# A transformer block with sixteen experts on one core: small operations moved to other places in the order, and permuted copies written contiguously

## The chip, the cores and the metric

The kernel runs on one core of a Trainium2 chip. The metric is the device time of one execution of the whole program, in microseconds (us); of several executions the median is given. A core has five engines that run side by side and wait for each other through semaphores: PE (the matrix engine, TensorE), DVE (VectorE), ACT (ScalarE), POOL (GpSimd) and SP (SyncE), which here issues nearly all transfers (DMAs) from the chip's memory. Matrix products land in PSUM, an accumulator memory that the program uses as eight banks of 128 x 512 floats; everything else lies in SBUF. Each engine works through its own instructions in the order in which the program has put them there, so an instruction that waits holds up all behind it on that engine.

## The reference

One block over 256 tokens of 1024 numbers, all in float32: a norm, one wide projection, two kinds of attention side by side, gates, an output projection, and then a mixture of experts. Cut to what matters:

```python
h = rms_norm(x, norm_mix_g)
(f_q, f_k, f_v, f_f, n_q, k_c, v_c, k_s, v_s, k_w, v_w, n_g, g_a, g_b) = split_cols(h @ w_in)   # 1024 x 4896
out_a = fox_attention(rms_norm(f_q), rms_norm(f_k), f_v, log_sigmoid(f_f + b_forget)) @ w_fox_up
kc = rms_norm(compress_blocks(k_c, ...))        # 15 blocks of 32 tokens, two layers with gelu
vc = compress_blocks(v_c, ...)
out_b = nsa_attention(rms_norm(n_q), kc, vc, rms_norm(k_s), v_s, rms_norm(k_w), v_w, sigmoid(n_g)) @ w_nsa_up
x = x + (sigmoid(g_a) * out_a + sigmoid(g_b) * out_b) @ w_out
...
# experts: 4 groups of 4; each token takes its best group, and the best two experts in it
hid = silu(einsum('td,edf->etf', t, w_gate)) * einsum('td,edf->etf', t, w_up)      # 1024 x 512 each
hid = hid * combine.T[:, :, None]
x = x + einsum('etf,efd->td', hid, w_down)                                         # 512 x 1024 each
```

The weights of the sixteen experts are 16 x 3 x 2 MB; each is read once.

## The kernel before

**Precision.** Before the experts, most operands are split into two parts, a rounded one (names with H) and the remainder (names with L), and a product is the sum of three products of parts. ACT makes the rounded part of a weight piece (`hi`, L173), DVE the remainder (`lo`, L179).

**Projection.** The weight matrix goes by in pieces of 2 x 512 columns. `go` issues half a piece's products (six matmuls on PE), `load` fetches a piece some steps ahead, and `hi` and `lo` split an earlier one. `half_a` is `go`, `lo`, `load` and then whatever functions it is given; `half_b` is `go`, `hi` and then its functions. So the functions of a `half_a` are issued behind a weight remainder on DVE. `k_scaled` (L753) is such a function: it scales the keys by their norms, twice, and `kk_turn` (L730) transposes the result on PE.

**Compressed keys and values.** `g_turn`, `c_in`, `c_root`, `c_turn`, `c_scores` and so on are short steps that are put between the attention's units. `c_in` forms keys and values of the compressed blocks in one PSUM bank, and ACT sums the keys' squares from there. `c_root` takes the root on DVE in a chain of small instructions, scales the keys (`kcn`, L836) and spreads the values over heads (`vblk`, L837), both out of that bank, which stays taken until then. `bank(...)` hands out banks by name; there are two of the name tp, in turn. An attention unit's scores are scaled by DVE (L579) and turned by PE (L587) into a bank tp.

**Tokens for the experts.** The tokens' rows are kept in permuted order as `xH` and `xL` (L1060 by ACT, L1063 by DVE; `by_row` and `eights` give the views): element q * 8 + k of a row goes to k * 128 + q, so that a slice of 128 columns is what one k step of a product wants. The products hid are permuted in the same way, by four.

**Experts' loop.** The experts go in eight pairs (here the first to the eighth; `pr` 0 to 7 in the code), each expert with up to 64 places for tokens, so that a pair fills the 128 columns of a product. `proj` (L1347) forms the gate or the up product of a pair: for each of eight k steps one matmul for either expert, and behind the fourth it calls the functions in `between`, half way. For each pair there are, in the order as written before:

- the gate product; half way through the up product `ready` for the next pair: one-hot matrices on DVE (L1007), `slots` (six small matmuls L1326 into a bank tp, and from it L1329 to L1331 on DVE, into `j6` and `csl`), and `rows` (two transposes and a copy of the one-hots on DVE, L1338 to L1340, in a bank tp too);
- `silu` on ACT (L1393, L1397), and the product hid on DVE (L1399), from the up product's bank;
- the scatter of the pair before (L1357, L1358) into four banks `acc` that hold the sum over all pairs;
- the turn: four transposes of hid (L1408) and their copy hdT on ACT (L1409);
- in every second pair the gather of the next two pairs' tokens (L1317, scaled by DVE, L1318);
- the down products (L1373), their results split into the parts of `y` by ACT and DVE (L1361, L1362);
- the issue of twelve more weight loads on SP;
- in the third and fifth pair four sums of `xH` and `xL` into `acc` on DVE (L1430), which add the block's input to the result.

The first pair's gate product is formed ahead of the loop. The second pair's `rows` and `ready` stand in its gate product's middle instead.

**Loads.** Expert weights come in tiles of 1 MB through SP's queue, first in, first out, into a ring of places; a load waits until the tile that lay in its place has been used, and the loads behind it wait with it.

**Order.** Within the loop the block `manual_schedule(engines={PE})` keeps PE's instructions as written; the order on DVE and ACT is chosen by the compiler's scheduler. For the eighth pair, `last_pair`, all engines keep the written order.

## Time and profile before

| | us |
|---|---|
| median of three runs | 451.19 |
| lowest and highest of them | 451.06, 453.54 |
| the profiled execution's own time | 451.66 |
| its span in the trace | 449.7 |
| PE busy in it | 430.3 |
| DVE busy in it | 214.7 |
| ACT busy in it | 167.0 |

The span is the stretch from the first recorded instruction to the last. Busy times are those in which an engine works; they overlap between engines. In rows of a timeline the first number is the start, in us from the span's start, the second the busy time of the row; then engine, line, operation, output<-inputs by the program's names, shapes, and the number of instructions that the row joins. A bracket at the end gives the idle time of the engine just ahead of the row and the instruction that ended it. In rows of groups, the numbers behind the bar are busy time in us, mean ns of one, and the idle time ahead of them with what ended most of it. The expert part of the program runs from some 225 us to the end.

### The profile page before, as it was taken

The page shows a single profiled execution, that of the slowest core. Times are in us where ns is not written, and L with a number is a line of the kernel's source. Part 1 is how long each engine was busy: PE and PEld are TensorE (multiplying, and loading weights), DVE is VectorE, ACT ScalarE, POOL GpSimd, SP SyncE. Part 2 cuts the span into 40 slices and gives each one's busy share as a digit, 9 for nine tenths or more (in the row PEclk, how much of TensorE's full clock was granted, in tenths as well). Part 3 has the DMA queues.
Part 4 walks back from the last instruction along what each step waited for, and adds up shares of the span by engine and source line. Part 5 has one row for each costly group of instructions (what it writes and reads, how often), then busy time and mean ns, then how long its engine had stood idle before and what let it go on. Part 6 is the DMA issues. An engine that isn't in the chain of part 4 may idle for free.

```text
span 449.7 us, 6356 instructions
## 1 busy us (share of the span) xinstructions
PE 430.3 (96%) x2370; PEld 258.9 (58%) x2370; DVE 214.7 (48%) x611; ACT 167.0 (37%) x343; POOL 10.5 (2%) x25
## 2 busy tenths in 40 slices
PE   7998999999999999999999899989999999999994
PEld 4895766767777777878952336333363335433443
DVE  5869776797856565576654224133130512201012
ACT  4786563957767665534732100101011010101011
POOL 8000000000000000000000000000000000000000
PEclk8999999999999999999999999999999999999998
DMA  8699643656763439999889999799999999999922
GB/s 285 131 366 303 216 138 95 222 183 214 254 206 94 129 109 351 408 408 374 352 310 335 351 391 422 280 422 421 420 420 418 420 420 418 422 418 416 391 78 98
DMA packets 41425, 136.10 MB, mean 303 GB/s; under 512 B 7296, under 2 KB 12976, under 8 KB 30384
## 3 DMA queue, kind: packets, MB, share of 16 engines
q1 hardware_dynamic: 41248, 135.54, 80.3%
q8 instruction: 20, 0.33, 0.3%
q10 hardware_dynamic: 144, 0.13, 0.1%
q14 instruction: 13, 0.11, 0.1%
HBM read 134.61 MB, written 1.05 MB: 302 GB/s over the span
## 4 chain that ended last, share of the span: by engine, by line


## 5 line engine op out<-in xcount | busy, mean ns | idle before, releaser
L1347 PE MATMUL z<-m,xg 128*64 128x512 f32 x432 | 100.5, 595 | 0.0
L179 DVE TENSOR_TENSOR wL<-raw,wH 128x1024 fp32r<-128x1024 f32 x48 | 58.4, 1220 | 12.2 <-ACT wH L173 12.0
L173 ACT ACTIVATE wH<-raw 128x1024 fp32r<-128x1024 f32 x48 | 50.5, 1056 | 36.8 <-PE z L201 21.5
L1347 PEld LDWEIGHTS z<-m,xg 128*64 128x64 f32 x432 | 31.5, 137 | 56.5 <-issue 54.6
L199 PE MATMUL z<-wH,hH 128*128 128x512 f32 x128 | 54.4, 425 | 0.0
L200 PE MATMUL z<-wL,hH 128*128 128x512 f32 x128 | 50.4, 393 | 0.0
L201 PE MATMUL z<-wH,hL 128*128 128x512 f32 x128 | 50.3, 393 | 0.0
L1373 PE MATMUL tp<-m,gh 128*64 128x512 f32 (+1 forms) x208 | 49.5, 580 | 0.7 <-ACT gh L1409 0.7
L1373 PEld LDWEIGHTS tp<-m,gh 128*64 128x64 f32 x208 | 15.8, 137 | 28.8 <-issue 25.7
L199 PEld LDWEIGHTS z<-wH,hH 128*128 128x128 f32 x128 | 24.1, 188 | 11.4 <-issue 7.1
L1361 ACT ACTIVATE y<-tp 128x512 fp32r<-128x512 f32 (+1 forms) x15 | 8.6, 583 | 56.7 <-PE tp L1373 56.6
L1340 DVE CAST ST<-tp 128x256 fp32r<-128x256 bf16 x8 | 3.4, 423 | 54.7 <-PE tp L1338 54.7
L1362 DVE TENSOR_TENSOR y<-tp,y 128x512 fp32r<-128x512 f32 (+1 forms) x15 | 10.0, 673 | 36.7 <-ACT y L1361 36.7
L201 PEld LDWEIGHTS z<-wH,hL 128*128 128x128 f32 x128 | 24.1, 188 | 5.5
L1409 ACT ACTIVATE gh<-tp 128x512 f32<-128x512 f32 x7 | 4.2, 598 | 59.6 <-PE tp L1408 59.6
L200 PEld LDWEIGHTS z<-wL,hH 128*128 128x128 f32 x128 | 24.2, 189 | 3.7
L570 ACT ACTIVATE sc<-sc,mx 128x128 f32<-128x128 f32 (+1 forms) x48 | 21.2, 445 | 1.7 <-DVE mx L564 1.4
L1393 ACT ACTIVATE gh<-z,csl 128x512 f32<-128x512 f32 x6 | 4.1, 688 | 39.2 <-PE z L1347 39.2
L1399 DVE SCALAR_TENSOR_TENSOR gh<-gh,csl,z 128x512 f32<-128x512 f32 x7 | 7.9, 1128 | 20.8 <-PE z L1347 15.1
L579 DVE TENSOR_SCALAR sc<-sc,sm 128x128 f32<-128x128 f32 (+1 forms) x48 | 12.1, 316 | 0.4
L1317 PE MATMUL tp<-one,xH 128*128 128x256 f32 x48 | 12.3, 297 | 0.0
L587 PE MATMUL tp<-ident,sc 128*128 128x128 f32 x72 | 10.5, 278 | 1.8 <-DVE vblk L837 1.0
(423 smaller groups left out, 701.5 us busy)
## 6 DMA issues: line engine op xcount, KB each, us to landing
m<-in_w_gate SPq DMA_DIRECT2D x29, 1024.0 KB, 17.2
m<-in_w_up SPq DMA_DIRECT2D x28, 1024.0 KB, 11.5
m<-in_w_down SPq DMA_DIRECT2D x22, 1024.0 KB, 12.5
raw<-in_w_in SPq DMA_DIRECT2D x36, 512.0 KB, 4.6
m<-in_w_down SPq DMA_DIRECT2D x10, 512.0 KB, 9.4
raw<-in_w_out SPq DMA_DIRECT2D x8, 512.0 KB, 10.3
m<-in_cmp_k_w SPq DMA_DIRECT2D x8, 256.0 KB, 8.5
m<-in_cmp_v_w SPq DMA_DIRECT2D x8, 256.0 KB, 4.8
```

Source lines behind the costliest of these rows:

```text
L173: A.activation(P["H"], P["raw"], AF.Copy)
L179: (eng or V).tensor_tensor(P["L"], P["raw"], P["H"].bitcast(F32), op=ALU.subtract)
L199: T.matmul(p[t], lH[k // 4][:, k % 4, ts], P["H"][:, k - k0], start=(k == 0), stop=False)
L200: T.matmul(p[t], lH[k // 4][:, k % 4, ts], P["L"][:, k - k0], start=False, stop=False)
L201: T.matmul(p[t], lL[k // 4][:, k % 4, ts], P["H"][:, k - k0], start=False, stop=(k == K - 1))
L570: A.activation(sc, sc, AF.Exp, scale=-1.0, bias=u["mx"][:, i, t:t + 1], accum_out=u["sm"][:, i, t:t + 1])
L579: V.tensor_scalar(sc, sc, u["sm"][:, i, t:t + 1], None, op0=ALU.mult)
L587: T.transpose(p[:, 128 * j:128 * j + 128], u["sc"][i][:, 128 * j:128 * j + 128], ident)
L1317: T.matmul(p[:, j], X[t][:, cs], Sr[:, t], start=(i == 0), stop=(i == 3))
L1347: T.matmul(p[64 * i:64 * i + 64], xg[:, k, o + 64 * i:o + 64 * i + 64], w[k // 4][:, k % 4], start=(k == 0), stop=(k == 7), tile_position= ...
L1362: V.tensor_tensor(yHL[:, 1, c0:c0 + n], p[:, 0:n], yHL[:, 0, c0:c0 + n].bitcast(F32), op=ALU.subtract)
L1373: T.matmul(p[64 * i:64 * i + 64, 0:n], hdT[:, f, 64 * i:64 * i + 64], w, start=(f == 0), stop=(f == 3), tile_position=(0, 64 * i))
```

## The change

It has six parts. Lines are those of the changed program where it says so.

1. `k_scaled` is issued ahead of the weight remainder instead of behind it.
2. In `c_in`, ACT copies the compressed keys out of the bank into a new tile `kcr`, and DVE forms `vblk` there; `c_root` then scales `kcr`, and no longer reads the bank.
3. The views of the permuted copies go the other way: the elements are visited in the order of the permuted tile, so it is written (or, in the sums into `acc`, read) contiguously, and the other operands, sums in PSUM among them, with a step of 8 or 4 floats. This concerns `xH`, `xL`, hid and the sums into `acc`. The same elements are computed.
4. `csl` and `j6` get two buffers each.
5. In the first pair the gate product of the second pair stands between hid and the down products, with the turn in its middle. The second pair then has only an up product in front of hid; `rows` of the first pair stands at its middle, and `ready` with `silu` of the second pair behind its sixth k step. The one-hots of the third pair are formed there too, but its `slots` and `rows` only behind the gather.
6. The loop's `manual_schedule` holds DVE and ACT in the written order as well.

```diff
@@ -766 @@
-        half_a(k_scaled)
+        go()
+        k_scaled()
+        lo()
+        load()
@@ c_in @@
-            p = pw[0] = bank([128, 512], "tp")
+            p = bank([128, 512], "tp")
...
             A.activation(ks_, p[0:32, 0:64], AF.Square, accum_out=kcst[:, 0:1])
+            A.activation(kcr, p[0:32, 0:64], AF.Copy)
+            V.tensor_tensor(vblk, p[:, None, 64:128].to_broadcast([128, 8, 64]), hm[:, :, None].to_broadcast([128, 8, 64]), op=ALU.mult)
@@ c_root @@
-            V.tensor_scalar(kcn, pw[0][0:32, None, 0:64].to_broadcast([32, 2, 64]), kcst[:, 1:2], None, op0=ALU.mult)
-            V.tensor_tensor(vblk, pw[0][:, None, 64:128].to_broadcast([128, 8, 64]), hm[:, :, None].to_broadcast([128, 8, 64]), op=ALU.mult)
+            V.tensor_scalar(kcn, kcr[:, None, :].to_broadcast([32, 2, 64]), kcst[:, 1:2], None, op0=ALU.mult)
@@ by_row, eights @@
-        return X.rearrange("p (k q) -> p q k", k=8)[:, c0 // 8:c1 // 8]
+        return X.rearrange("p (k q) -> p k q", k=8)[:, :, c0 // 8:c1 // 8]
...
-        return X[:, c0:c1].rearrange("p (q k) -> p q k", k=8)
+        return X[:, c0:c1].rearrange("p (q k) -> p k q", k=8)
@@ slots @@
-        c = wk.tile([128, 3], F32, name="csl")
-        j6 = wk.tile([128, 6], F32, name="j6")
+        c = wk.tile([128, 3], F32, name="csl", bufs=2)
+        j6 = wk.tile([128, 6], F32, name="j6", bufs=2)
@@ proj @@
-    def proj(w0, w1, xg, o, between=()):
+    def proj(w0, w1, xg, o, between=(), after=()):
...
+            if k == 5:
+                for f in after:
+                    f()
@@ expert_pair @@
-        if pr:
-            pg = proj(tiles[2 * pr, 0], tiles[2 * pr + 1, 0], xg, o, pre0)
-            pre0.clear()
+        if pr == 1:
+
+            pu = proj(tiles[2, 1], tiles[3, 1], xg, o, pre0, [lambda: (pre.append(ready(1)()), silu(pg0[1], pre[0][0])),
+                                                               lambda: later.append(ready(2))])
+            c, Sb, ST = pre.pop(0)
+        elif pr:
+            pg = proj(tiles[2 * pr, 0], tiles[2 * pr + 1, 0], xg, o)
             c, Sb, ST = pre.pop()
-            A.activation(sg, pg, AF.Silu, scale=c[:, 1:2])
-        pu = proj(tiles[2 * pr, 1], tiles[2 * pr + 1, 1], xg, o, [lambda: pre.append(ready(pr + (pr > 0))())])
-        if pr == 0:
+            silu(pg, c)
+            pu = proj(tiles[2 * pr, 1], tiles[2 * pr + 1, 1], xg, o, [lambda: pre.append(ready(pr + 1)())])
+        else:
+            pu = proj(tiles[0, 1], tiles[1, 1], xg, o, [lambda: pre.append(ready(0)())])
             c, Sb, ST = pre.pop()
-            A.activation(sg, pg0, AF.Silu, scale=c[:, 1:2])
-        fours = lambda h: h.rearrange("p (q k) -> p q k", k=4)
-        V.scalar_tensor_tensor(hid.rearrange("p (k q) -> p q k", k=4), fours(sg), c[:, 2:3], fours(pu), op0=ALU.mult, op1=ALU.mult)
+            silu(pg0[0], c)
+        fours = lambda h: h.rearrange("p (q k) -> p k q", k=4)
+        V.scalar_tensor_tensor(hid.rearrange("p (k q) -> p k q", k=4), fours(sg), c[:, 2:3], fours(pu), op0=ALU.mult, op1=ALU.mult)
...
+        if pr == 0:
+            pg0.append(proj(tiles[2, 0], tiles[3, 0], xg, 128, [turn]))
+        else:
+            turn()
...
         if pr % 2 == 1:
             xgs[pr // 2 + 1] = gather(pr // 2 + 1)
+        if later:
+            pre.append(later.pop()())
...
-                        o = acc[t][hf].rearrange("p (q k) -> p q k", k=8)
+                        o = acc[t][hf].rearrange("p (q k) -> p k q", k=8)
...
-            pre0.extend([lambda: got.append(rows(Sb)), lambda: pre.append(ready(1)())])
+            pre0.append(lambda: got.append(rows(Sb)))
@@ the loop @@
-    with tc.manual_schedule(engines={mybir.EngineType.PE}):
+    with tc.manual_schedule(engines={mybir.EngineType.PE, mybir.EngineType.DVE, mybir.EngineType.Activation}):
```

How the instructions stand on an engine in the two programs, at three places; a name with a number is one tile of that name, and x2 or x4 joins equal rows.

On DVE at the compressed keys, before, from the copy of the hidden layer to the next weight remainder; `kcst` and `rs_u` are the root's small tiles, `sm` and `sc` those of an attention unit's softmax:

```order
L808 TENSOR_SCALAR hT<-tp_843 128x128
L809 COPY hTv<-hT 128x256
L573 RECIPROCAL sm<-sm 128x4
L575 TENSOR_TENSOR sm<-sm,ngate 128x4
L579 TENSOR_SCALAR sc<-sc,sm 128x128
...
L834 TENSOR_SCALAR kcst<-kcst 32x1
...
L836 TENSOR_SCALAR kcn<-tp_859,kcst 32x128
L837 TENSOR_TENSOR vblk<-tp_859,hm 128x512
L179 TENSOR_TENSOR wL<-raw,wH 128x1024
```

And in the changed program:

```order
L810 TENSOR_SCALAR hT<-tp_844 128x128
L811 COPY hTv<-hT 128x256
L179 TENSOR_TENSOR wL<-raw,wH 128x1024
L821 TENSOR_TENSOR vblk<-tp_860,hm 128x512
L573 RECIPROCAL sm<-sm 128x4
L575 TENSOR_TENSOR sm<-sm,ngate 128x4
L579 TENSOR_SCALAR sc<-sc,sm 128x128
...
L839 TENSOR_SCALAR kcst<-kcst 32x1
```

`vblk` now stands ahead of the attention unit's scaling, and the last reader of its bank is no longer behind the root's chain.

On PE in the first pair, before: z is the bank of a gate or up product, m and wl are weight tiles, gh is the tile that holds sg, hid and hdT, and tp a bank for turns and down products.

```order
L1347 MATMUL z_2670<-m_2033,xg 64x512
L1347 MATMUL z_2670<-m_2055,xg 64x512
L1408 MATMUL tp_2704<-ident,gh 128x128 x4
L1373 MATMUL tp_2711<-m_2077,gh 64x512
L1373 MATMUL tp_2711<-m_2099,gh 64x512
...
L1347 MATMUL z_2761<-m_2121,xg 64x512
L1347 MATMUL z_2761<-m_2145,xg 64x512
```

And in the changed program:

```order
L1351 MATMUL z_2672<-m_2035,xg 64x512
L1351 MATMUL z_2672<-m_2057,xg 64x512
L1351 MATMUL z_2706<-m_2123,xg 64x512
L1351 MATMUL z_2706<-m_2147,xg 64x512
...
L1427 MATMUL tp_2715<-ident,gh 128x128 x4
L1351 MATMUL z_2706<-m_2176,xg 64x512
L1351 MATMUL z_2706<-m_2207,xg 64x512
...
L1380 MATMUL tp_2730<-m_2079,gh 64x512
L1380 MATMUL tp_2730<-m_2101,gh 64x512
```

Half of the second pair's gate product (eight matmuls) now stands on each side of the turn; the down products follow behind its second half.

On DVE in the third pair, before: `ST` is the copy of `rows`, one_3095 the one-hots of the fourth pair, gh<-gh,csl,z the product hid, and o and s banks of `acc`.

```order
L1340 CAST ST<-tp_2989 128x256
L1007 TENSOR_TENSOR one_3095<-slot,rank__2607 128x128 x2
L1399 SCALAR_TENSOR_TENSOR gh<-gh,csl,z_2965 128x128x4
L1430 TENSOR_TENSOR o_2663<-o_2663,xH_2221 128x512
L1329 ISA j_2985,csl<-tp_2977,half 128x6
L1329 ISA csl 128x1
L1330 TENSOR_REDUCE csl<-tp_2977 128x1
L1430 TENSOR_TENSOR o_2663<-o_2663,xL_2222 128x512
L1331 TENSOR_TENSOR csl<-csl 128x1
```

And in the changed program:

```order
L1333 ISA j_2987,csl<-tp_2979,half 128x6
L1333 ISA csl 128x1
L1334 TENSOR_REDUCE csl<-tp_2979 128x1
L1335 TENSOR_TENSOR csl<-csl 128x1
L1344 CAST ST<-tp_2991 128x256
L1416 SCALAR_TENSOR_TENSOR gh<-gh,csl,z_2967 128x512
L1369 TENSOR_TENSOR y<-tp_3020,y 128x512
L1369 TENSOR_TENSOR y<-tp_3031,y 128x512
L1456 TENSOR_TENSOR o_2665<-o_2665,xH_2223 128x8x64
L1456 TENSOR_TENSOR o_2665<-o_2665,xL_2224 128x8x64
```

The reads of `slots`'s bank (`j6` and `csl`) moved from behind hid to ahead of it, and the sums into `acc` from between them to behind the parts of `y`; the fourth pair's one-hots now stand behind those sums.

More of the change, by code (lines that the diff above doesn't have):

```diff
@@ L801, in block_kernel @@
         hTv = at.tile([128, 2, 2, 4, 16], F32, name="hTv")
-        pw = {}
         def g_turn():
@@ L831, in block_kernel @@
         ks_ = wk.tile([32, 64], F32, name="kcs", bufs=1)
+        kcr = wk.tile([32, 64], F32, name="kcr", bufs=1)
         def c_root():
@@ L1385, in ready, with silu @@
         return rest_
+    def silu(pg, c):
+        A.activation(sg, pg, AF.Silu, scale=c[:, 1:2])
+    pg0, later = [pg0], []
     def expert_pair(pr, pend):
         xg, o = xgs[pr // 2], pr % 2 * 128
-        if pr:
-            pg = proj(tiles[2 * pr, 0], tiles[2 * pr + 1, 0], xg, o, pre0)
-            pre0.clear()
+        if pr == 1:
[4 more added lines that the diff above has]
+            pg = proj(tiles[2 * pr, 0], tiles[2 * pr + 1, 0], xg, o)
             c, Sb, ST = pre.pop()
-            A.activation(sg, pg, AF.Silu, scale=c[:, 1:2])
-        pu = proj(tiles[2 * pr, 1], tiles[2 * pr + 1, 1], xg, o, [lambda: pre.append(ready(pr + (pr > 0))())])
-        if pr == 0:
+            silu(pg, c)
+            pu = proj(tiles[2 * pr, 1], tiles[2 * pr + 1, 1], xg, o, [lambda: pre.append(ready(pr + 1)())])
+        else:
+            pu = proj(tiles[0, 1], tiles[1, 1], xg, o, [lambda: pre.append(ready(0)())])
             c, Sb, ST = pre.pop()
-            A.activation(sg, pg0, AF.Silu, scale=c[:, 1:2])
-        fours = lambda h: h.rearrange("p (q k) -> p q k", k=4)
-        V.scalar_tensor_tensor(hid.rearrange("p (k q) -> p q k", k=4), fours(sg), c[:, 2:3], fours(pu), op0=ALU.mult, op1=ALU.mult)
+            silu(pg0[0], c)
+        fours = lambda h: h.rearrange("p (q k) -> p k q", k=4)
+        V.scalar_tensor_tensor(hid.rearrange("p (k q) -> p k q", k=4), fours(sg), c[:, 2:3], fours(pu), op0=ALU.mult, op1=ALU.mult)
         if pr == 1:
@@ L1405, in expert_pair, with turn @@
             scatter(*pend, 512, 512, pr == 1)
-        p = bank([128, 4, 128], "tp")
-        for f in range(4):
-            T.transpose(p[:, f], hid[:, f * 128:f * 128 + 128], ident)
-        A.activation(hdT, p, AF.Copy)
+        def turn():
+            p = bank([128, 4, 128], "tp")
+            for f in range(4):
+                T.transpose(p[:, f], hid[:, f * 128:f * 128 + 128], ident)
+            A.activation(hdT, p, AF.Copy)
+        if pr == 0:
+            pg0.append(proj(tiles[2, 0], tiles[3, 0], xg, 128, [turn]))
+        else:
+            turn()
         if pend and pr % 2 == 0:
```

## The prediction

> **What bounds it now.** First the page's busy shares, then its clock and bandwidth rows, to see which engine could set the end at all.
>
> ```profile
> span 449.7 us, 6356 instructions
> PE 430.3 (96%) x2370; PEld 258.9 (58%) x2370; DVE 214.7 (48%) x611; ACT 167.0 (37%) x343; POOL 10.5 (2%) x25
> PEclk8999999999999999999999999999999999999998
> GB/s 285 131 366 303 216 138 95 222 183 214 254 206 94 129 109 351 408 408 374 352 310 335 351 391 422 280 422 421 420 420 418 420 420 418 422 418 416 391 78 98
> ```
>
> PE is busy 96% at the full clock, so time is won only where PE stands still, or by doing less on it; this change takes nothing off PE. The bandwidth stands flat near 420 GB/s from slice 26 (292 us) on, so the weights might set the end instead. The DMA view by stretches gives 15.1 us from issue to landing for the last pieces of the eighth pair's up weights; the timeline gives the issue and the use:
>
> ```profile
> m<-in_w_up SPq DMA_DIRECT2D x3, 512.0 KB, 15.1
> 405.19 0.33 SPq L107 DMA_DIRECT2D m<-in_w_up  x1
> 429.47 1.03 PE L1450 MATMUL z<-m,xg 128*64 128x256 f32 x8
> ```
>
> The piece lands at 405.2 + 15.1 = 420.3 and is used at 429.5: 9.2 us of slack. PE, not the DMA, sets the end, and up to about 9 us can be taken from PE before weights are late. So I went through PE's timeline for rows with idle time in brackets. Behind 40 us there are few; these are the ones near the edited lines:
>
> ```profile
> 42.84 0.66 PE L730 MATMUL tp<-ident,m 128*128 128x128 f32 x4 [1.16 <-DVE m L753]
> 67.67 0.52 PE L587 MATMUL tp<-ident,sc 128*128 128x128 f32 x3 [1.05 <-DVE vblk L837]
> 228.82 0.36 PE L1213 MATMUL s<-one,xH 128*128 128x256 f32 x1 [1.08 <-DVE one L1007]
> 247.89 0.66 PE L1408 MATMUL tp<-ident,gh 128*128 128x128 f32 x4 [1.28 <-DVE gh L1399]
> 249.23 1.94 PE L1373 MATMUL tp<-m,gh 128*64 128x512 f32 x8 [0.69 <-ACT gh L1409]
> 260.69 0.48 PE L1326 MATMUL tp<-cb,one 128*128 128x3 bf16 x6 [0.72 <-DVE one L1007]
> 302.38 0.63 PE L1408 MATMUL tp<-ident,gh 128*128 128x128 f32 x4 [1.27 <-DVE csl L1330]
> 354.60 0.63 PE L1408 MATMUL tp<-ident,gh 128*128 128x128 f32 x4 [0.55 <-DVE csl L1330]
> 406.80 0.63 PE L1408 MATMUL tp<-ident,gh 128*128 128x128 f32 x4 [0.53 <-DVE csl L1330]
> ```
>
> They sum to 8.33 us, and the change touches all nine. A wait costs about 0.1 us more than its bracket, since an unhindered matmul starts before the modelled end of the last.
>
> **The change, part by part.**
>
> *(a) The scaled keys ahead of the weight remainder.* At 42.84 PE waits for the two L753 products, which stand behind an L179:
>
> ```profile
> 40.37 1.22 DVE L179 TENSOR_TENSOR wL<-raw,wH 128x1024 fp32r<-128x1024 f32 x1
> 41.50 1.29 DVE L753 TENSOR_TENSOR m<-kraw,krs 128x512 f32<-128x512 f32 x2
> ```
>
> Swapped, the products end at about 41.7, where PE comes free (42.84 - 1.16 = 41.68). Left is some 0.15 for the handover: 1.16 + 0.1 - 0.15 = **1.1 us** gained. The L179 ends 1.3 us later; its piece is consumed two pieces on, so nobody waits. The load behind it waits for an older remainder.
>
> *(b) The compressed keys and values.* At 67.67 the second turn waits for a PSUM bank that `c_root` still reads:
>
> ```profile
> 62.81 0.66 PE L816 MATMUL tp<-w,hTv 128*128 128x64 f32 x4
> 63.61 1.01 DVE L579 TENSOR_SCALAR sc<-sc,sm 128x128 f32<-128x128 f32 x4
> 63.74 0.18 ACT L817 ACTIVATION_READ_ACCUMULATOR kcs<-tp 32x1 f32 x1
> 66.13 0.49 PE L587 MATMUL tp<-ident,sc 128*128 128x128 f32 x3
> 66.85 0.67 DVE L837 TENSOR_TENSOR vblk<-tp,hm 128x512 f32<-128x512 f32 x1
> 72.32 1.07 PE L851 MATMUL tp<-nqT,kcT 64*32 64x256 f32 x16
> ```
>
> Now ACT copies the keys (a 32-row copy, some 0.2 us as its square beside it) and DVE forms vblk straight behind it, 64.15 to 64.85. The bank is free 2.7 us sooner. But vblk now stands ahead of the score scaling, and what is behind it on DVE waits: scaling ends near 66.3 instead of 64.62. PE's second turn would start near 66.45, so it just fits. The root chain, the next remainder and the next scores move 0.6 us later; PE, 1.15 us earlier, meets them at the compressed scores (72.32), where I leave 0.15. Gain 1.05 + 0.1 - 0.15 = **1.0 us**.
>
> *(c) xH and xL, hid, and the sums into acc: contiguous writes, strided reads.* Their present prices, and the contiguous neighbour:
>
> ```profile
> L1399 DVE SCALAR_TENSOR_TENSOR gh<-gh,csl,z 128x512 f32<-128x512 f32 x7 | 7.9, 1128 | 20.8 <-PE z L1347 15.1 <-issue 5.7
> L1063 DVE TENSOR_TENSOR xL<-x,xH 128x512 fp32r<-128x512 f32 x4 | 4.2, 1078 | 0.6 <-ACT xH L1060 0.6
> L1430 DVE TENSOR_TENSOR s<-s,xH 128x512 f32<-128x512 f32 x2 | 2.1, 1050 | 0.3 <-PE s L1358 0.3
> L1362 DVE TENSOR_TENSOR y<-tp,y 128x512 fp32r<-128x512 f32 x14 | 9.6, 690 | 36.7 <-ACT y L1361 36.7
> ```
>
> L1399 has one strided side, the write. L1430 has one too, but it is a read (xH; acc and output are contiguous), and costs as much. L1063 has both and still costs 1.08. So a stride costs about 0.4 us whichever side has it, and not twice. No row shows a read with a step of 4 or 8 floats, nor any strided PSUM operand. The price therefore lies between 0.69 (the step is free) and 0.69 + 2 x 0.44 = 1.57 us (hid's two strided inputs add up). I take **unchanged**, 1.13 and 1.05: L1430 is the nearest row, being a strided read. Then the wait at 228.82, behind two L1063 (2 x 1.08) and a one-hot, stays: **0**. At 0.69 it gives 2 x 0.39 = 0.78.
>
> The Trainium skill, Vector Engine (DVE) Microarchitecture Reference, section 5.2, speaks against the edit: it measured streams that hop every element at about 1.7 ns a column and small steps of 24 words at 2.5, with "more for small non-adjacent steps than for large ones". By its figures hid would take an estimated 512 x 2.5 + 75 ns = 1.36 us and the whole sum below would be near 4.8 us. The strided L1399 here comes to 1128 / 512 = 2.2 ns a column all in, with a step of 128 words; nothing here shows a small step.
>
> *(d) First pair.* The second pair's gate product is put behind hid, with the turn in its middle.
>
> ```profile
> 246.75 1.08 DVE L1399 SCALAR_TENSOR_TENSOR gh<-gh,csl,z 128x512 f32<-128x512 f32 x1 [3.25 <-PE z L1347]
> 248.59 0.60 ACT L1409 ACTIVATE gh<-tp 128x512 f32<-128x512 f32 x1 [4.50 <-PE tp L1408]
> 256.15 3.60 PE L1347 MATMUL z<-m,xg 128*64 128x512 f32 x16
> ```
>
> The last row is half a product (four of eight k): 3.44 us without its tail. hid (1.1) now runs beside the first half and the hdT copy (0.60 plus handover) beside the second; even at 1.57 hid is covered. Both waits go: 1.28 + 0.69 + 0.2 = **2.2 us**. The same matmuls are done. If that cover were gone, the two waits would be back whole. The SP queue keeps its order; the first pair's down slots come free about 2.5 us later in it and hold the loads queued behind, out of a slack of 9.
>
> *(e) Second pair.* The wait for a one-hot at 260.69 goes, because four k steps' half (1.7 us) now lies between the cast and it: +0.72 + 0.1. In its place `slots` and `rows` of the third pair now follow the gather and use the same two banks. `rows` waits for the gather's last scaling and the down product for the j6 reads:
>
> ```profile
> L1318 DVE TENSOR_TENSOR xg<-tp,g_row 128x512 f32<-128x512 f32 x12 | 8.3, 691 | 7.9 <-PE tp L1317 7.9
> 302.07 0.16 DVE L1330 TENSOR_REDUCE csl<-tp 128x1 f32<-128x3 f32 x1
> ```
>
> Scaling ends 0.15 + 0.69 behind the gather, `slots` covers 0.3: 0.6 with handover, then 0.2 for the reads. Lost 0.8; net **0**.
>
> *(f) Third, fifth and seventh pair.* j6 and csl stood behind hid (single buffer), at the third behind an acc sum as well, and the turn needs their bank:
>
> ```profile
> 300.12 1.13 DVE L1399 SCALAR_TENSOR_TENSOR gh<-gh,csl,z 128x512 f32<-128x512 f32 x1 [2.85 <-issue]
> 300.71 0.40 PE L1358 MATMUL s<-y,ST 128*128 128x512 f32 x1
> ```
>
> With two buffers and DVE in written order they run before hid; only hid is left. It ends at 301.25, PE could go at 300.71 + 0.23: 0.35 left with handover, at each of three. 1.27 + 0.55 + 0.53 + 0.3 - 3 x 0.35 = **1.6 us**; at hid 0.69 all 2.65, at 1.57 some 0.3.
>
> *(g) Written order on DVE.* At the fourth and sixth pair the one-hots now queue behind four acc sums:
>
> ```profile
> 310.78 7.04 PE L1347 MATMUL z<-m,xg 128*64 128x512 f32 x32
> 311.65 0.69 DVE L1362 TENSOR_TENSOR y<-tp,y 128x512 fp32r<-128x512 f32 x1 [2.77 <-ACT y L1361]
> ```
>
> From 310.78: y ends at 1.56, four sums 4.2, one-hots 0.55, ready at 6.3. PE asks after a product and a half, 6.9 + 3.44 = 10.3. Hidden, cost **0**; it shows once a sum takes over 2.05 us.
>
> Sum: 1.1 + 1.0 + 0 + 2.2 + 0 + 1.6 + 0 = **5.9 us**. The profiled execution took 451.66 (span 449.7 and 2.0 around it), 0.47 over the median 451.19; 451.66 - 5.9 = 445.8 for it, 445.3 for the median.
>
> **Rivals.**
> - *Small-step reads are nearly free* (0.69): (c) gives 0.78, (f) 2.65; sum 7.7, 443.5 us. For: the new steps are 16 and 32 bytes instead of 512. Against: L1430.
> - *They are dearer* (1.57): (f) shrinks to 0.3, sum 4.6, 446.6 us; this is also where the skill's figure points. For: hid now has two strided inputs, one in PSUM. Against: L1063's two sides do not add.
> - *The early gains are given back*: (b) puts 0.7 us ahead of a scaling with 0.1 us to spare, and DVE re-meets PE late at several units before 120 us. Without (a) and (b), 3.8 us and 447.4.
> - *Slower*: strided PSUM on both sides of the acc sums. No row shows one. At 3.2 us each (three times now), (g)'s chain ends at 1.56 + 12.8 + 0.55 = 14.9 against 10.3: 4.6 lost twice, 9.2 - 5.9 = 3.3 slower, 454.5. It decides from 2.05 us, and the net turns to a loss from 2.8.
> - That the order doesn't move as meant is excluded: the program's listing shows the moves.
>
> **Numbers.** Forecast 0.50 (444.6 to 446.2 its own range), cheap reads 0.18, dear reads 0.12, early gains lost 0.16, slower 0.04. The range 443.0 to 448.0 reaches to cheap reads and to the lost gains. About 1% (4.5 us, to 446.7) is what a measurement tells from no change. Faster by more: 0.50 + 0.18 + half of the dear case, 0.74; within: the rest of it and the lost gains, 0.22; slower 0.04.
>
> **What would show it.** (a), (b): no bracket at the L730 and second L587 turns. (c): mean of hid against 1128, of the acc sums against 1050. (d): no idle at the first pair's turn or down. (e): a new bracket of 0.6 at `rows` behind the second pair's gather. (f): brackets near 0.2 named after hid, not csl. (g): none at the fourth and sixth pair's `slots`. Wrong if the late weights appear as PE waits on DMA, if the clock row falls below 9 in the expert slices, or if hid's mean exceeds 1.6.

## The result, and the profile after

The changed kernel takes 445.02 us (median of four runs, 444.37 to 446.13), beside 451.88 for the kernel before (four runs, 451.06 to 453.54; the three of them that stand ahead of the prediction have a median of 451.19). The ratio is 0.985, with a 95% interval of 0.981 to 0.989: 1.5% faster. The prediction said 445.3 us, from 443.0 to 448.0. The profiled execution took 444.37 us, with a span of 442.3; before it was 449.7. So 7.4 us have gone from the span, where the sum of the prediction had 5.9.

First the same rows of the page of the profile, then the clock in a window that the prediction did not look at: PE's granted clock (1.00 is full speed) is the number behind POOL's.

```profile
span 442.3 us, 6352 instructions
...
PE 428.2 (97%) x2370; PEld 257.0 (58%) x2370; DVE 211.9 (48%) x611; ACT 167.3 (38%) x344; POOL 10.6 (2%) x25
...
PEclk9999999999999999999999999999999999999999
```

Stretch from 8 to 13 us, before:

```profile
8.00:13.00 5.00, 4.78 (x16) 3.62 (x17) 4.60 (x20) 3.50 (x9) 2.90 (x4) 0.66 1.08 372
```

The same stretch after:

```profile
8.00:13.00 5.00, 4.38 (x23) 2.94 (x23) 4.91 (x20) 4.19 (x10) 3.01 (x4) 1.00 1.08 364
```

In the profile of before the clock stood at 0.66 over these 5 us, 5 x 0.34 = 1.7 us of lost work; after it was full. Nothing of the change has run by then, and at 38 us before is 0.99 us behind. So the two spans can't be compared as they are; what the change did is read from a place just ahead of its first effect. PE's timeline gives such places. After:

```profile
38.04 1.07 PE L693 MATMUL o<-m,m 128*32 128x256 f32 x16
...
40.78 0.66 PE L730 MATMUL tp<-ident,m 128*128 128x128 f32 x4
...
69.03 1.07 PE L855 MATMUL tp<-nqT,kcT 64*32 64x256 f32 x16
...
225.56 0.36 PE L1217 MATMUL s<-one,xH 128*128 128x256 f32 x1 [1.20 <-DVE one L1011]
...
226.67 3.65 PE L1234 MATMUL z<-m,xg 128*64 128x512 f32 x16
...
272.82 0.27 PE L1342 MATMUL tp<-identb,one 128*128 128x128 bf16 x2 [0.63 <-DVE xg L1322]
...
294.30 0.50 PE L1364 MATMUL o<-y,ST 128*128 128x512 f32 x1
...
295.69 0.66 PE L1427 MATMUL tp<-ident,gh 128*128 128x128 f32 x4 [0.20 <-DVE gh L1416]
...
347.58 0.66 PE L1427 MATMUL tp<-ident,gh 128*128 128x128 f32 x4 [0.20 <-DVE gh L1416]
...
399.45 0.66 PE L1427 MATMUL tp<-ident,gh 128*128 128x128 f32 x4 [0.17 <-DVE gh L1416]
```

And the three of before that the prediction does not show:

```profile
39.03 1.07 PE L693 MATMUL o<-m,m 128*32 128x256 f32 x16
...
229.94 2.37 PE L1230 MATMUL z<-m,xg 128*64 128x512 f32 x10
...
299.92 0.50 PE L1357 MATMUL o<-y,ST 128*128 128x512 f32 x1
```

The differences of these starts are the gain, place by place:

| place on PE | before | after | ahead by | gained since the row above | predicted |
|---|---|---|---|---|---|
| L693, ahead of the first edit | 39.03 | 38.04 | 0.99 | (0.99, no edit) | |
| turn of the keys | 42.84 | 40.78 | 2.06 | 1.07 | (a) 1.1 |
| compressed scores | 72.32 | 69.03 | 3.29 | 1.23 | (b) 1.0 |
| first gate product | 229.94 | 226.67 | 3.27 | -0.02 | (c) 0 |
| scatter in the third pair | 299.92 | 294.30 | 5.62 | 2.35 | (d), (e) 2.2 |
| turn in the third pair | 302.38 | 295.69 | 6.69 | 1.07 | (f) |
| turn in the fifth pair | 354.60 | 347.58 | 7.02 | 0.33 | (f) |
| turn in the seventh pair | 406.80 | 399.45 | 7.35 | 0.33 | (f) 1.6 for the three |

The change itself is worth 7.35 - 0.99 = 6.36 us between the first and the last place; 5.9 were predicted. From the last place to the end nothing is added (7.4 at the end). In these rows PE still waits five times. The 1.20 us is the one-hot's wait, 1.08 before; the 0.63 is new; 0.20, 0.20 and 0.17 are left of the waits at the three turns. The other five of the nine waits that the prediction showed are gone.

The prices of the operations that were given other views, in the groups of after:

```profile
L1416 DVE SCALAR_TENSOR_TENSOR gh<-gh,csl,z 128x512 f32<-128x512 f32 x7 | 7.9, 1134 | 19.8 <-PE z L1351 15.2 <-DMA m<-in_w_gate 3.6 <-issue 0.9
...
L1067 DVE TENSOR_TENSOR xL<-x,xH 128x512 fp32r<-128x512 f32 x4 | 4.5, 1140 | 0.6 <-ACT xH L1064 0.6
...
L1456 DVE TENSOR_TENSOR s<-s,xL 128x512 f32<-128x512 f32 x2 | 1.4, 699 | 0.1
...
L1456 DVE TENSOR_TENSOR s<-s,xH 128x512 f32<-128x512 f32 x2 | 1.4, 688 | 0.0
```

The product hid is where it was (1134 ns for 1128), xL is a little dearer (1140 for 1078), which the one-hot's wait behind two of them shows (1.20 for 1.08), and the sums into `acc`, which now hop in PSUM instead of SBUF, cost 690 ns for 1050.

### The profile page after: what moved, and what is told of

It is laid out like the page before. It is cut to its first block, busy times and chain, and to the rows that moved or that the text cites. A ratio compares the mean times of both kernels' runs of the same rounds, so it can differ in the third digit from the quotient of the medians.

```text
span 442.3 us, 6352 instructions
## 1 busy us (share of the span) xinstructions
PE 428.2 (97%) x2370; PEld 257.0 (58%) x2370; DVE 211.9 (48%) x611; ACT 167.3 (38%) x344; POOL 10.6 (2%) x25
## 3 DMA queue, kind: packets, MB, share of 16 engines
HBM read 134.61 MB, written 1.05 MB: 307 GB/s over the span
## 4 chain that ended last, share of the span: by engine, by line
## 5 line engine op out<-in xcount | busy, mean ns | idle before, releaser
L1333 DVE CUSTOM_DVE_ANT_0 j<-tp,half 128x6 f32<-128x6 f32 x8 | 1.3, 163 | 43.1 <-PE tp L1330 43.1
L1416 DVE SCALAR_TENSOR_TENSOR gh<-gh,csl,z 128x512 f32<-128x512 f32 x7 | 7.9, 1134 | 19.8 <-PE z L1351 15.2
L1321 PE MATMUL tp<-one,xL 128*128 128x256 f32 x48 | 11.9, 282 | 0.0
```

The source lines that it names most:

```text
L1321: T.matmul(p[:, j], X[t][:, cs], Sr[:, t], start=(i == 0), stop=(i == 3))
```

## The experiments

The start of the program differs from run to run by up to 2.4 us. So for each run two things are given: the measured time, and a stretch, from the start of the second L693 group on PE to the start of the turn in the seventh pair. It is 399.45 - 38.04 = 361.41 us in the changed kernel and 406.80 - 39.03 = 367.77 before.

| run | time, us | ratio to before (95%) | L693 | turn, 7th pair | stretch | against after |
|---|---|---|---|---|---|---|
| after | 445.02 | 0.981 to 0.989 | 38.04 | 399.45 | 361.41 | |
| after_again | 445.23 | 0.984 to 0.987 | 38.99 | 400.46 | 361.47 | +0.06 |
| undo_early | 447.98 | 0.988 to 0.995 | 38.48 | 402.32 | 363.84 | +2.43 |
| undo_pairs | 449.68 | 0.991 to 0.995 | 38.38 | 402.57 | 364.19 | +2.78 |
| undo_layout | 445.15 | 0.983 to 0.989 | 38.32 | 399.65 | 361.33 | -0.08 |
| one_buffer | 446.75 | 0.985 to 0.992 | 38.76 | 401.79 | 363.03 | +1.62 |
| undo_order | 445.28 (one run) | | 38.73 | 400.26 | 361.53 | +0.12 |
| layout_alone | 453.33 (one run) | | 38.70 | 408.12 | 369.42 | (before: +1.65) |
| silu_permuted | 444.26 | 0.978 to 0.987 | 38.24 | 398.59 | 360.35 | -1.06 |
| slots_in_gate | 444.93 (one run) | | 38.70 | 399.63 | 360.93 | -0.48 |
| rest_split | 444.09 (one run) | | 38.15 | 399.32 | 361.17 | -0.24 |
| all_three | 444.30 | 0.980 to 0.984 | 40.42 | 400.08 | 359.66 | -1.75 |

The changed kernel taken twice agrees within 0.06 us in the stretch, so differences of a few tenths can be read there that the times can't show. Where one run is all there is, the time has no interval.

### The two early edits undone

```diff
-        go()
-        k_scaled()
-        lo()
-        load()
+        half_a(k_scaled)
...
-            A.activation(kcr, p[0:32, 0:64], AF.Copy)
...
-            V.tensor_scalar(kcn, kcr[:, None, :].to_broadcast([32, 2, 64]), kcst[:, 1:2], None, op0=ALU.mult)
+            V.tensor_scalar(kcn, pw[0][0:32, None, 0:64].to_broadcast([32, 2, 64]), kcst[:, 1:2], None, op0=ALU.mult)
+            V.tensor_tensor(vblk, pw[0][:, None, 64:128].to_broadcast([128, 8, 64]), hm[:, :, None].to_broadcast([128, 8, 64]), op=ALU.mult)
```

> The changed kernel with its first two parts undone: the scaled keys again behind the weight remainder, and vblk and the keys read from the bank by the root step again. My theory (terms a and b of the sum): the brackets ahead of the key turn and of the second score turn come back at about 1.15 and 1.05 us, and the time is 2.1 to 2.3 us above the changed kernel, a ratio of about 0.990 to the kernel before. Rival (the early gains are given back by units before 120 us): the brackets come back but the experts start less than 0.5 us later, ratio 0.985.

PE's timeline of this kernel has both waits again, to a few hundredths as they were before:

```profile
42.31 0.66 PE L730 MATMUL tp<-ident,m 128*128 128x128 f32 x4 [1.18 <-DVE m L753]
...
67.12 0.52 PE L587 MATMUL tp<-ident,sc 128*128 128x128 f32 x3 [1.05 <-DVE vblk L837]
```

The stretch is 2.43 us longer, and the time 3.0 us. The rival falls: what is gained before 70 us is kept to the end.

### The order of the first two pairs undone

```diff
-        if pr == 1:
-            pu = proj(tiles[2, 1], tiles[3, 1], xg, o, pre0, [...])
...
+        if pr:
+            pg = proj(tiles[2 * pr, 0], tiles[2 * pr + 1, 0], xg, o, pre0)
+            pre0.clear()
...
-        if pr == 0:
-            pg0.append(proj(tiles[2, 0], tiles[3, 0], xg, 128, [turn]))
-        else:
-            turn()
+        turn()
...
-            pre0.append(lambda: got.append(rows(Sb)))
+            pre0.extend([lambda: got.append(rows(Sb)), lambda: pre.append(ready(1)())])
```

> The changed kernel with the order of the first two pairs undone: the second pair's gate product is formed in the second pair again, the turn stands right behind hid, and slots and rows of the third pair stand in the second pair's up product. My theory (terms d and e): the brackets ahead of the first pair's turn and down products come back at 1.2 to 1.3 and 0.69 us, the bracket of 0.63 us ahead of rows behind the gather goes, the one-hot's bracket of about 0.7 in the second pair comes back; the time is about 2.2 us above the changed kernel, ratio 0.989 to 0.990. Rival (the written order on DVE and the two buffers do the work, the pairs' order nothing): within 0.5 us of the changed kernel, ratio 0.985.

The first pair on DVE and PE, and the one-hot's wait in the second:

```profile
240.04 3.65 PE L1351 MATMUL z<-m,xg 128*64 128x512 f32 x16
...
244.18 1.12 DVE L1412 SCALAR_TENSOR_TENSOR gh<-gh,csl,z 128x512 f32<-128x512 f32 x1 [3.60 <-PE z L1351]
...
245.36 0.66 PE L1423 MATMUL tp<-ident,gh 128*128 128x128 f32 x4 [1.66 <-DVE gh L1412]
...
246.70 1.51 PE L1380 MATMUL tp<-m,gh 128*64 128x512 f32 x6 [0.69 <-ACT gh L1424]
...
258.16 0.48 PE L1330 MATMUL tp<-cb,one 128*128 128x3 bf16 x6 [0.72 <-DVE one L1011]
```

All three waits are back and the one ahead of `rows` is gone. The stretch is 2.78 us longer, where 2.2 were expected. The surplus is at the turn, which waits 1.66 us instead of 1.28. The up product's second half ends at 240.04 + 3.65 = 243.69 and hid starts 0.49 us behind it. Before, it ended at 246.61 (its row is the one below) and hid started at 246.75, 0.14 behind.

```profile
242.96 3.65 PE L1347 MATMUL z<-m,xg 128*64 128x512 f32 x16
```
 
In the changed kernel hid starts 0.50 us behind that product as well (243.84 behind 243.34), and the profile puts the end of the wait down to a transfer:

```profile
243.84 1.15 DVE L1416 SCALAR_TENSOR_TENSOR gh<-gh,csl,z 128x512 f32<-128x512 f32 x1 [3.60 <-DMA m<-in_w_gate]
```

Two runs that are described further down tell what brings the 0.35 us. Both keep the changed order of the pairs and leave the order on DVE and ACT to the scheduler; undo_order first, then one_buffer:

```profile
244.25 1.15 DVE L1416 SCALAR_TENSOR_TENSOR gh<-gh,csl,z 128x512 f32<-128x512 f32 x1 [3.25 <-PE z L1351]
...
244.30 1.15 DVE L1416 SCALAR_TENSOR_TENSOR gh<-gh,csl,z 128x512 f32<-128x512 f32 x1 [3.25 <-DMA m<-in_w_gate]
```

In both, hid starts 0.14 us behind the product (which ends at 244.11 and 244.16), though the profile names the same transfer in one_buffer. In all ten traces with the written order the distance is 0.49 to 0.50 us, in all four without it 0.14 or 0.15. So hid's later start comes with the written order (part 6) and not with a transfer; which wait the written order adds there stays open. In the changed kernel the gate product behind hid hides it, here it shows.

The ten times of this kernel fall into two groups: four from 447.7 to 448.5 us, with a mean granted clock of 0.997 or 0.998, and six from 449.7 to 450.3, with 0.989 to 0.994. The profiled execution (447.84) is one of the four. So the stretch, 2.8 us, measures the edit better than the medians, which differ by 4.7.

### The layout undone, and the layout alone

```diff
-        return X.rearrange("p (k q) -> p k q", k=8)[:, :, c0 // 8:c1 // 8]
+        return X.rearrange("p (k q) -> p q k", k=8)[:, c0 // 8:c1 // 8]
...
-        fours = lambda h: h.rearrange("p (q k) -> p k q", k=4)
+        fours = lambda h: h.rearrange("p (q k) -> p q k", k=4)
```

(and in the same way in `eights`, hid and the sums; layout_alone makes the opposite edit in the kernel before)

> The changed kernel with the old views for xH, xL, hid and the sums into acc (strided writes of hid, xH and xL; strided reads of xH and xL in the sums). The trace after shows hid at 1134 ns for 1128 before, xL at 1140 for 1078, the sums at 694 for 1055. My theory (a stride in SBUF costs about 0.4 us on either side, one in PSUM nothing): the sums go back to 1.05 us each, hid stays at 1.13, xL falls to 1.08; the sums are hidden, so the time is that of the changed kernel within 0.3 us, or 0.1 us shorter by xL, ratio 0.984 to 0.985. Rival (the layout carries part of the gain): 0.5 us or more above it.

> The kernel before with the new views alone. My theory (strides in SBUF 0.4 us on either side, in PSUM nothing): the sums into acc go from 1.05 to 0.69 us, hid stays at 1.13, xL rises from 1.08 to 1.14; of the brackets only the third pair's turn changes, where one sum stands ahead of csl: from 1.27 to 1.0. All others as before, the span within 0.5 us of before, apart from the first 25 us. Rival (the layout is what the change brings): hid falls and the turn's brackets fall with it.

The groups with the layout undone, in the otherwise changed kernel:

```profile
L1416 DVE SCALAR_TENSOR_TENSOR gh<-gh,csl,z 128x512 f32<-128x512 f32 x7 | 7.9, 1132 | 19.7 <-PE z L1351 18.8 <-issue 0.9
...
L1456 DVE TENSOR_TENSOR s<-s,xL 128x512 f32<-128x512 f32 x2 | 2.1, 1054 | 0.1
```

The sums cost 1.05 us again and hid as before; xL falls to 1.08, the one-hot's wait to 1.08, and the stretch is 0.08 us shorter. The part that gives the change its name is worth nothing in time, as the prediction had it.

Alone, the layout shows where it could matter: the third pair's turn, where a sum stands ahead of `csl`, waits 1.01 us instead of 1.27. Yet this run was longer than before by 1.65 us in the stretch, against the expectation. The windows of it, from the first pair's turn on, show why:

```profile
247.00:249.00 2.00, 0.66 (x4) 0.42 (x4) 0.73 (x1) 0.52 (x1) 0.00 (x0) 1.00 1.06 395
249.00:251.00 2.00, 1.87 (x8) 0.69 (x10) 0.00 (x0) 0.07 (x1) 0.00 (x0) 0.77 0.96 389
251.00:253.00 2.00, 2.00 (x8) 0.58 (x6) 0.00 (x0) 0.00 (x0) 0.00 (x0) 0.50 0.97 397
253.00:255.00 2.00, 2.00 (x10) 0.62 (x8) 0.00 (x0) 0.00 (x0) 0.00 (x0) 0.88 0.69 287
```

The granted clock was halved for a while: 2 x (0.23 + 0.50 + 0.12) = 1.7 us lost. Without it the stretch is that of the kernel before, to 0.1 us. The clock fell just behind a time in which PE mostly stood still: in the first of these windows it was busy for 0.66 of 2 us, because of the first pair's waits (1.31 and 0.69 us here).

### One buffer, and the scheduler's order

```diff
-        c = wk.tile([128, 3], F32, name="csl", bufs=2)
-        j6 = wk.tile([128, 6], F32, name="j6", bufs=2)
+        c = wk.tile([128, 3], F32, name="csl")
+        j6 = wk.tile([128, 6], F32, name="j6")
...
-    with tc.manual_schedule(engines={mybir.EngineType.PE, mybir.EngineType.DVE, mybir.EngineType.Activation}):
+    with tc.manual_schedule(engines={mybir.EngineType.PE}):
```

(undo_order makes the last edit alone)

> The changed kernel with one buffer each for csl and j6, and the order on DVE and ACT left to the scheduler (only PE held as written); one buffer in the written order can't be had, since csl would wait for a product that stands behind it. My theory (term f): the turn's brackets at the third, fifth and seventh pair are again those of a csl that stands behind hid, about 0.55 at the fifth and seventh and 0.9 at the third (one sum at 0.69 instead of 1.05 stands between), for 0.20, 0.20 and 0.17 now: 1.4 us above the changed kernel, ratio 0.988. Rival (DVE is not late there, the gain came with the pairs' order): no change, ratio 0.985.

> The changed kernel with the order on DVE and ACT in the experts' loop left to the scheduler, csl and j6 with two buffers. The scheduler puts the third pair's j6 and csl ahead of hid by itself once there are two buffers. My theory (term f came by the buffers, not by the written order): brackets at the turns 0.20, 0.20 and 0.17 as in the changed kernel, span the same within 0.3 us apart from the first 25 us. Rival (the written order does it): the third pair's bracket, with sums and one-hots ahead of hid, is 0.5 us or more.

The three turns with one buffer:

```profile
297.34 0.63 PE L1427 MATMUL tp<-ident,gh 128*128 128x128 f32 x4 [1.04 <-DVE csl L1334]
...
349.57 0.63 PE L1427 MATMUL tp<-ident,gh 128*128 128x128 f32 x4 [0.57 <-DVE csl L1334]
...
401.79 0.63 PE L1427 MATMUL tp<-ident,gh 128*128 128x128 f32 x4 [0.54 <-DVE csl L1334]
```

With two buffers, and the same freedom for the scheduler:

```profile
296.45 0.66 PE L1427 MATMUL tp<-ident,gh 128*128 128x128 f32 x4 [0.20 <-DVE gh L1416]
```

and 0.20 and 0.17 at the other two. The run with one buffer is 1.62 us longer than the changed kernel, the scheduler's order alone 0.12, so one buffer costs 1.50 us. The term (f) measured 1.73; the 0.23 between them is the third turn, which waits 1.04 us here and 1.27 before, because the sum ahead of `csl` costs 0.69 us in the new layout. With two buffers nothing of that is left to gain, so the second buffer alone does the work of the term (f). The written order on DVE and ACT by itself is worth a tenth of a microsecond at most.

### What a stride costs on DVE

Twelve additions in the fourth pair, into a part of gh that nothing reads. `by` visits 512 floats with a step of k, `ct` without one; a0 and b0 lie in SBUF, u0 in PSUM.

```diff
+            V.tensor_tensor(g3, a0, b0, op=ALU.add)
+            V.tensor_tensor(ct(g3, 2), by(a0, 2), ct(b0, 2), op=ALU.add)
+            V.tensor_tensor(ct(g3, 4), by(a0, 4), ct(b0, 4), op=ALU.add)
+            V.tensor_tensor(ct(g3, 8), by(a0, 8), ct(b0, 8), op=ALU.add)
+            V.tensor_tensor(ct(g3, 16), by(a0, 16), ct(b0, 16), op=ALU.add)
+            V.tensor_tensor(ct(g3, 4), by(a0, 4), by(b0, 4), op=ALU.add)
+            V.tensor_tensor(by(g3, 4), ct(a0, 4), ct(b0, 4), op=ALU.add)
+            V.tensor_tensor(g3, u0, b0, op=ALU.add)
+            V.tensor_tensor(ct(g3, 4), by(u0, 4), ct(b0, 4), op=ALU.add)
...
```

> The changed kernel with twelve additions of 128 x 512 floats on DVE in the fourth pair, into a part of the tile gh that nothing reads; they leave the output alone and only their prices matter. Theory A (a stride costs about 0.4 us in SBUF on either side, not twice, and nothing in PSUM): contiguous 0.69; first input in SBUF read with a step of 2, 4, 8 and 16 floats 1.05 to 1.15 each, both inputs with a step of 4 no more than that, a write with a step of 128 floats the same; from PSUM contiguous 0.69, with a step of 4 or 16 floats 0.69, PSUM contiguous and SBUF with a step of 4 1.1. Theory B (what decides is the size of the step, whichever memory): steps of 2 and 4 cheap or of their own price, PSUM with a step of 4 as dear as SBUF, 1.1.

The answer by source line, in the order above (ns, least, median and greatest of one):

```profile
L1451 DVE TENSOR_TENSOR gh<-xH,xL x1: 681/681/681, 333.9 to 333.9; 128x512 f32<-128x512 f32 x1
...
L1452 DVE TENSOR_TENSOR gh<-xH,xL x1: 692/692/692, 334.7 to 334.7; 128x512 f32<-128x512 f32 x1
...
L1453 DVE TENSOR_TENSOR gh<-xH,xL x1: 1100/1100/1100, 335.4 to 335.4; 128x512 f32<-128x512 f32 x1
...
L1454 DVE TENSOR_TENSOR gh<-xH,xL x1: 1089/1089/1089, 336.5 to 336.5; 128x512 f32<-128x512 f32 x1
...
L1455 DVE TENSOR_TENSOR gh<-xH,xL x1: 1023/1023/1023, 337.6 to 337.6; 128x512 f32<-128x512 f32 x1
...
L1456 DVE TENSOR_TENSOR gh<-xH,xL x1: 1102/1102/1102, 338.7 to 338.7; 128x512 f32<-128x512 f32 x1
...
L1457 DVE TENSOR_TENSOR gh<-xH,xL x1: 1122/1122/1122, 339.8 to 339.8; 128x512 f32<-128x512 f32 x1
...
L1459 DVE TENSOR_TENSOR gh<-z,xL x1: 691/691/691, 341.7 to 341.7; 128x512 f32<-128x512 f32 x1
```

In SBUF a step of 2 floats is free (692 beside 681), a step of 4, 8 or 16 costs 0.34 to 0.42 us (1100, 1089, 1023), two such inputs no more than one (1102), and a write the same (1122). That write, `by(g3, 4)`, has a step of 4 floats, and not of 128 as the expectation says; the write with a step of 128 is hid's in the kernel before, 1128. From PSUM a step of 4 is free (691); a contiguous PSUM input measured 692, one with a step of 16 floats 691, and a contiguous PSUM input beside an SBUF input with a step 1051. Theory A holds but for the step of 2, which it had at the full price. The time of this run (450.84 us) says nothing, since the additions stand in the way of the pairs behind them.

The step of 2 has a rule. The Trainium skill, SBUF — State Buffer, Door 1 (The DMA port swizzle), in its note on cachelines, says that SBUF is read in lines of 16 bytes and that two hits on a line are needed for full bandwidth. A step of 2 floats hits each line twice, one of 4 once: the runs agree, 692 and 1100 ns. The same note has a stride of 4 floats still free; here it costs 0.4 us, and the measurement decides. The note's sentence on PSUM (lines of 8 bytes, at a cost to matmuls) does not show on DVE here.

### Three further edits, alone and together

In silu_permuted, ACT writes sg in the permuted order:

```diff
-        A.activation(sg, pg, AF.Silu, scale=c[:, 1:2])
+        A.activation(sg.rearrange("p (k q) -> p k q", k=4), pg.rearrange("p (q k) -> p k q", k=4), AF.Silu, scale=c[:, 1:2])
...
-        V.scalar_tensor_tensor(hid.rearrange("p (k q) -> p k q", k=4), fours(sg), c[:, 2:3], fours(pu), op0=ALU.mult, op1=ALU.mult)
+        V.scalar_tensor_tensor(hid.rearrange("p (k q) -> p k q", k=4), sg.rearrange("p (k q) -> p k q", k=4), c[:, 2:3], fours(pu), op0=ALU.mult, op1=ALU.mult)
```

> The changed kernel with sg written by ACT in the permuted order already (read from PSUM with a step of 4 floats), so that hid reads sg contiguously and only its PSUM operand with a step. Theory A (steps in PSUM are free on DVE): hid falls from 1134 to about 690 ns, the turn's brackets at the third, fifth and seventh pair (0.20, 0.20, 0.17) go, the first pair's and the last are as now; 0.6 us less from the third pair on, ratio about 0.983 to 0.984. Theory B (the small step costs in PSUM too): hid stays at 1.1 us and nothing moves. If ACT pays for the step in PSUM instead, silu rises from 687 to about 1100 ns, which the up product of 7 us hides.

The groups of silu_permuted:

```profile
L1416 DVE SCALAR_TENSOR_TENSOR gh<-gh,csl,z 128x512 f32<-128x512 f32 x7 | 5.2, 747 | 19.7 <-PE z L1351 18.8 <-issue 0.9
...
L1395 ACT ACTIVATE gh<-z,csl 128x512 f32<-128x512 f32 x7 | 4.8, 689 | 41.0 <-PE z L1351 31.4 <-DVE csl L1334 5.0 <-PE tp L1330 4.5
```

With the hop only in PSUM, hid falls from 1134 to 747 ns, and ACT pays nothing for reading PSUM with a step (689 ns for 687). The three brackets at the turns are gone; the stretch is 1.06 us shorter, 0.35 for each turn. That is more than the 0.6 expected, which were the brackets alone.

In slots_in_gate the small products and turns of the third pair move into its gate product:

```diff
-        if later:
-            pre.append(later.pop()())
...
-            pg = proj(tiles[2 * pr, 0], tiles[2 * pr + 1, 0], xg, o)
+            pg = proj(tiles[2 * pr, 0], tiles[2 * pr + 1, 0], xg, o, [lambda: pre.append(later.pop()())] if later else ())
```

> The changed kernel with slots and rows of the third pair in the middle of that pair's gate product instead of behind the gather. My theory (term e): rows waits behind the gather because both stand in line for the same two banks; half a product of 3.4 us behind the down products covers the reads, so the bracket of 0.63 us ahead of rows goes and nothing comes for it: 0.6 to 0.7 us less from there on. Rival (a new wait): silu needs csl right behind the gate product, rows waits for the down product's parts; a bracket of 0.3 us or more at the third pair's gate or up product.

The wait ahead of `rows` goes and none comes for it, but the stretch gains 0.48 us rather than 0.6; what takes the rest is not shown.

In rest_split the second half of xL comes behind the one-hots:

```diff
-        for c in (0, 512):
-            xrest(1, c, c + 512)
+        xrest(1, 0, 512)
...
         onehot(Sr, 1, 0, 4)
+        xrest(1, 512, 1024)
```

> The changed kernel with the one-hots of the second half of the tokens put on DVE between the two halves of xL (1.14 us each), instead of behind both. My theory: the wait of 1.20 us ahead of the gather's second half is that of the one-hots behind two strided xL; with one of them ahead it falls to about 0.1, and the second xL then comes late by some 0.3 to 0.6 us at the fifth k step or at the scaling behind it: net 0.5 to 0.8 us less. Rival (the rank's matmul is what comes late): the bracket stays above 0.8.

PE's timeline of rest_split:

```profile
224.62 0.36 PE L1216 MATMUL s<-one,xH 128*128 128x256 f32 x1 [0.19 <-DVE one L1011]
225.52 0.39 PE L1217 MATMUL s<-one,xL 128*128 128x256 f32 x1 [0.54 <-DVE xL L1067]
```

The one-hot's wait falls from 1.20 to 0.19, and 0.54 of it comes back 0.9 us later for the second xL; the stretch gains 0.24 us, half of the least that was expected.

In all_three the three edits stand together, and after_again is the changed kernel once more, on the same chip.

> The changed kernel with three edits: sg written permuted (as in silu_permuted, which took the three turn brackets away, 0.7 us), slots and rows of the third pair moved into that pair's own gate product, and the one-hots of the second half of the tokens put between the two halves of xL. My theory: what PE waits for is additive here, so 0.7 + 0.6 + 0.5 = 1.8 us less than the changed kernel, some 443.2 us for its 445.0, ratio to before 0.980 to 0.981. Rival (a wait that is taken away comes back at the next meeting): the gain stays that of silu_permuted, 0.7 us.

> The changed kernel once more, beside all_three on the same chip: 445.0 us, ratio to before 0.984 to 0.985; the brackets as in its first profile.

The three gains add up in the trace, 1.06 + 0.48 + 0.24 = 1.78 for 1.75 measured. That the expected 1.8 was met is luck as far as its terms go: it had 0.7, 0.6 and 0.5. In the times it is less clear: 444.30 for 445.23 on the same chip, and the intervals 0.980 to 0.984 and 0.984 to 0.987 touch. The profiled execution of all_three had its clock at half in the first microseconds:

```profile
8.00:13.00 5.00, 4.64 (x13) 3.45 (x14) 4.22 (x18) 3.04 (x9) 2.61 (x4) 0.50 1.07 382
```

Its L693 starts 2.4 us later than in the first profile of the changed kernel, and so eats the gain. Its lowest run is 442.99, the lowest of the changed kernel 444.37. It is the quickest of the kernels in the stretch; by its times alone that would not be settled.

## Why the prediction was right

**(a), (b).** Predicted 1.1 and 1.0; the places give 1.07 and 1.23. Of (b), the 0.15 that were left for a wait at the compressed scores did not come: their row in after has no bracket. DVE's rows of after show the steps:

```profile
39.43 1.29 DVE L753 TENSOR_TENSOR m<-kraw,krs 128x512 f32<-128x512 f32 x2
...
61.99 0.69 DVE L821 TENSOR_TENSOR vblk<-tp,hm 128x512 f32<-128x512 f32 x1 [1.32 <-ACT kcr L820]
...
63.00 1.00 DVE L579 TENSOR_SCALAR sc<-sc,sm 128x128 f32<-128x128 f32 x4
```

The products end at 40.72, 0.06 us ahead of the turn. `vblk` does stand ahead of the scaling, which ends at 64.0, just as PE begins its turns (64.06, with no wait in the timeline). The cover of 0.1 us that the prediction counted on held. The rival that the early gains are given back is refuted by undo_early.

**(c).** The sum of 0 was right (-0.02 measured); the price of one of its operations was not. The prediction took the sums into `acc` as unchanged at 1.05, since L1430 was a strided read. They cost 0.69: what L1430 paid for was the step in SBUF, and the new step is in PSUM. The traces of before had no strided PSUM operand that could have told, and the prediction said so. Nothing came of it, because the sums are hidden: with the layout undone they cost 1.05 and the stretch is the same. For hid the value taken was right, 1.13, since its input sg still hops in SBUF (747 ns when it no longer does), and the PSUM input's step does not add. Both rivals on its price fall with that: neither 0.69 nor 1.57. The figure of the Trainium skill (Vector Engine (DVE) Microarchitecture Reference, 5.2), an estimated 1.36 us for hid, is above the 1.13 us measured. The slower rival needed 2.05 us for a sum; it falls too.

**(d), (e).** Predicted 2.2 net, measured 2.35. The three waits went, and the new one ahead of `rows` is 0.63, predicted 0.6; the further 0.2 for the reads does not show as a wait. Undoing the part takes 2.78, 0.4 more, because the written order on DVE and ACT starts hid of the first pair 0.35 us later, which the new order of the pairs hides. The prediction has no term for that.

**(f).** Predicted 1.6, measured 1.73 with brackets of 0.20, 0.20 and 0.17, predicted near 0.2 and named after hid. Only the attribution was too wide: the prediction gave the gain to the two buffers and the written order together, and the buffers alone do it.

**(g).** No wait at the fourth and sixth pair; hidden, as predicted.

The terms sum to 6.36 for 5.9, all but (a) and (c) being a little larger. That the median fell by 6.9 and the profiled span by 7.4 is more than the change: 0.99 us of the span lay ahead of the first edit, in an execution of before with its clock down at the start. The prediction read the clock row of before, whose first digit is 8, but made nothing of it. The medians move with the runs that make them up: from the 451.19 that the prediction started from, the fall is 6.2 us. Times of one kernel spread by about 2 us here, so that 445.02 met 445.3 within 0.3 us is partly luck; what bears the prediction out is the gain place by place.

## What to carry to other kernels

List PE's waits in order of time and price each by what the waiting instruction will wait for next; here nine small waits, each less what is late next, gave the gain to half a microsecond. Where two forms of an operation differ in their strides, ask first in which memory the hop lies: in these runs a permutation cost nothing where DVE or ACT read the data from PSUM and SBUF stayed contiguous (silu_permuted). A small tile with one buffer can hold up a whole bank; here a second buffer took that wait away under either order on DVE.

## What the runs showed of the hardware that was not expected

- On DVE, 128 x 512 floats: a step of 4 to 16 floats in SBUF 1.02 to 1.12 us, a step of 2 floats 0.69, steps in PSUM 0.69. ACT reading PSUM with a step of 4 floats: 0.69, as without.
- PE's granted clock falls to half for a short stretch in some executions: at the start in five of the fourteen traces (0.66 in the window of 5 us in before, 0.50 in all_three), at 250 us in layout_alone and at 345 us in strides. One such stretch costs about 1.7 us of PE's work, and the longer ones of all_three and strides about 3.4, more than most edits here are worth. The Trainium skill, TensorE: Matmul & The Clock Gate, What's actually happening, has the clock halved or full by windows of 3413 ns: half of that is 1.7 us, and the loss measured in layout_alone agrees.
- In these traces the clock fell only just behind a time in which PE stood still. In layout_alone it was the first pair's waits, 1.31 and 0.69 us; in strides this one, from the additions:

```profile
345.48 0.49 PE L1330 MATMUL tp<-cb,one 128*128 128x3 bf16 x6 [2.56 <-DVE one L1011]
```

At the start, the five traces with a fallen clock show waits of 1.30 to 2.41 us ahead of the row of L303 on PE, the other nine 0.33 to 1.32. Such a wait does not always bring it: behind 1.28 and 0.69 us in the first pair, before keeps its full clock. Since the change takes these two waits away, it may spare some executions the 1.7 us as well; no run shows how often.
